# Four sums of operands per pair of row tiles, on GpSimd instead of VectorE

## The chip, the cores and the metric

The kernel runs on one NeuronCore of a Trainium2 chip. The metric is the device time of one execution in microseconds (us). A core has five engines that run their own instruction queues in order and wait for each other by semaphores: TensorE (PE; its weight loads are shown as PEld), VectorE (DVE), ScalarE (ACT), GpSimd (POOL) and SyncE (SP). TensorE writes its results to the banks of PSUM; the other data lies in SBUF.

## The reference, cut to what matters

One decoder layer in float32 over 512 tokens with 1024 channels: a convolution branch and a gated linear attention branch, merged and projected, and then the channel mixer, in which the change lies. There, 1024 channels are projected to 2 x 2816, each of these columns is convolved over time with three taps, the first half goes through silu and is multiplied by the second, and the product is projected back to 1024.

```python
u2 = _rmsnorm(h, norm2_g[l])
z = _causal_dwconv(u2 @ w_ffn_up[l], ffn_dw_w[l], ffn_dw_b[l])
h = h + (jax.nn.silu(z[..., :FFN_DIM]) * z[..., FFN_DIM:]) @ w_ffn_down[l]
return _rmsnorm(h, final_g)
```

## The kernel before

**Precision.** TensorE multiplies in a format with fewer bits than float32, so each operand is split in two: ScalarE copies it to a high part, and VectorE subtracts that from the operand to give the low part. Three matmuls (`mm3`, L309 to L311) then make one product. Weights are split in `split_weight` (copy at L239 or L266, subtraction at L240 or L267; tiles raw, whi, wlo), and the products of the channel mixer in `fsplit` (L1096, L1097; tiles yh and yl, ah and al, sh and sl).

**The channel mixer** goes through 22 row tiles of 128 hidden channels, two by two: 11 pairs in three groups of 4, 3 and 4 pairs (`GROUPS`, L34). For each row tile two up-projections of 24 matmuls fill one PSUM bank each (`col_tile`). `ffn_conv` takes a bank: a bias pass on ScalarE (L1081), and two taps on VectorE (L1083). `glu` multiplies the two halves on VectorE (L1091), to the tile w for the first of a pair and to f for the second.

**Seven products.** The down-projection of a group is not done as eight products of half blocks but as seven, in the manner of Strassen and Winograd, from sums of operands. With w = (w1, w2) and f = (f1, f2), halves of 256 tokens, the sums on the side of the activations are w1 - w2 (L1104), s1 = w2 - f2 (L1114), n2 = s1 - w1 (L1115) and s4 = f1 + n2 (L1116). The first lies in the last third of the tile w, the other three in the tile v. `first_of_pair` splits w1 and w1 - w2 in one copy and one subtraction (yh, yl), and `second_of_pair` splits f (ah, al) and then all of v (sh, sl).

**The products of a group** are made by `seven`, in the order of `STEPS` (L46): a11, a11, a12, s1, a12, s1, then n2, s4, n3 and a22 with two blocks each. The number behind a step picks the first two pairs or the rest of the group. Steps a11 and n3 read y, a12 and a22 read a, and s1, n2 and s4 read s. So the s of a group's last pair is first read in the second block of s1, and its y in the second block of a11. After a step's last block VectorE adds the PSUM bank to the residual (hres, L1019).

**The weights of the seven products** are sums too: `operand` adds one block to another on VectorE (L218), and on GpSimd's queue transfers are issued that accumulate a block from HBM onto a tile (L225 once the tile's split is done, L208 once the tile's first load has landed). SyncE issues the plain loads. Weights are split up to two steps ahead (`LOOK`), in four buffers each for raw, whi and wlo.

**Order.** Outside the start, a scheduler orders each engine's queue when the program is built, by the order in which instructions were written and by when it takes them to be ready. So a line of later code can stand ahead of an earlier one on the same engine. At run time each queue is strictly in order.

GpSimd does few other things: memsets at the start, the roots of the norms (L357, L460, L1152, L1153) and the accumulating transfers.

Of the kernel before, what the change touches and what calls it, by code (L numbers as in the profile page):

```python
# [15 lines left out]
ALU = mybir.AluOpType  # L16
# [3 lines left out]
T = 512  # L20
# [46 lines left out]
def trunk_layer(ctx: ExitStack, tc: tile.TileContext, a: dict, out: bass.AP):  # L67
    nc = tc.nc
# [23 lines left out]
    def nm(s):  # L92
        return f"{s}_{next(names)}"
# [836 lines left out]
    H = T // 2  # L930
# [18 lines left out]
    for p, q in O_PAIRS:  # L949
# [6 lines left out]
        s1, n2, n3, s4 = e1[:, :H], e1[:, H:], e2[:, :H], e2[:, H:]  # L956
# [129 lines left out]
    def glu(i, accs, out):  # L1086

        za = ffn_conv(accs[0], i)
        nc.scalar.activation(za, za, AF.Silu)
        zb = ffn_conv(accs[1], FT + i)  # L1090
        nc.vector.tensor_tensor(out, za, zb, ALU.mult)  # L1091

    def fsplit(src, n, tag):
        hi, lo = (fp.tile([P, n], F32R, tag=tag + p, name=nm(tag + p), bufs=4) for p in "hl")
        shaped = (lambda x: x.rearrange("p (c t) -> p c t", t=H)) if len(src.shape) == 3 else (lambda x: x)
        nc.scalar.copy(shaped(hi), src)  # L1096
        nc.vector.tensor_tensor(shaped(lo), src, shaped(hi).bitcast(F32), ALU.subtract)  # L1097
        return lambda c, n=1: tuple(x[:, c * H : (c + n) * H] for x in (hi, lo))

    def first_of_pair(i, accs):  # L1100

        w = fp.tile([P, 3 * H], F32, tag="w", name=nm("w"), bufs=2)
        glu(i, accs, w[:, :T])
        nc.vector.tensor_tensor(w[:, T:], w[:, :H], w[:, H:T], ALU.subtract)  # L1104
        y = fsplit(w.rearrange("p (c t) -> p c t", t=H)[:, 0:3:2, :], T, "y")
        return w, {"a11": y(0), "n3": y(1)}

    def second_of_pair(i, accs, w, acts):

        f = fp.tile([P, T], F32, tag="f", name=nm("f"), bufs=2)  # L1110
        glu(i, accs, f)
        v = fp.tile([P, 3 * H], F32, tag="v", name=nm("v"), bufs=2)
        s1, n2, s4 = (v[:, c * H : (c + 1) * H] for c in range(3))
        nc.vector.tensor_tensor(s1, w[:, H:T], f[:, H:], ALU.subtract)  # L1114
        nc.vector.tensor_tensor(n2, s1, w[:, :H], ALU.subtract)  # L1115
        nc.vector.tensor_tensor(s4, f[:, :H], n2, ALU.add)  # L1116
        y = fsplit(f, T, "a")
        acts["a12"], acts["a22"] = y(0), y(1)
        y = fsplit(v, 3 * H, "s")
        acts["s1"], acts["n2"], acts["s4"] = y(0), y(1), y(2)  # L1120
        return acts
# [64 lines left out]
    for gi, pairs in enumerate(GROUPS):  # L1186
        acts = []
        early = {}
        if gi == 0:

            ws = [weight("w_up", j, 0) for i in pairs[0] for j in (i, FT + i)]
            accs = [mm_bank() for _ in ws]
            for lo in (0, T // 2):
                for j, (w, acc) in enumerate(zip(ws, accs)):
                    col_tile(w, acts2, acc, lo, lo + T // 2)
                    if lo == 0 and j in (1, 2):
                        to_channels(normed[j + 1], u2, j + 1)
            early = {pairs[0][0]: accs[:2], pairs[0][1]: accs[2:]}

        def both(i):  # L1200
            return early.get(i) or [col_tile(weight("w_up", i), acts2), col_tile(weight("w_up", FT + i), acts2)]

        for p, q in pairs:
            w, found = first_of_pair(p, both(p))
            acts.append(second_of_pair(q, both(q), w, found))
        if gi < len(GROUPS) - 1:
            seven("w_down", pairs, acts, lambda t, n, c: None)
        else:
            seven("w_down", pairs, acts, last_complete, last_at, True)
# [90 lines left out]
```

## Time and profile before

| what | us |
|---|---|
| median of 3 runs | 837.96 |
| lowest and highest of them | 837.56, 837.98 |
| the profiled execution | 837.74 |
| its span, first to last instruction | 836.0 |
| the channel mixer's up-projections and seven products | about 494 to 826 of the span |
| busy in that stretch: TensorE, VectorE, ScalarE, GpSimd | 332.0, 244.5, 154.1, 17.4 |
| the four sums, 44 instructions on VectorE | 18.7 busy (4.7, 4.7, 4.7, 4.6) |

The granted TensorE clock was 0.999 of full speed over the span. A line of the profile's timeline gives the start, the duration, the engine, the line of the kernel, the operation and the tiles (output, arrow, inputs) with their shapes; the time that an engine stood idle before an instruction stands in brackets, with what it waited for. VectorE and TensorE overlap the end of an instruction with the next one's beginning, so what an instruction takes of its queue is the distance of two starts, which is a little less than its duration.

### The profile page before, as it was taken

What the parts mean: (1) busy time and instruction counts of PE and PEld (TensorE: products, weight loads), DVE (VectorE), ACT (ScalarE), POOL (GpSimd) and SP (SyncE); (2) the same over time, 40 slices, a digit from 0 to 9 for tenths busy, and PEclk for the clock granted to TensorE, in tenths of its full rate; (3) what the DMA queues carried; (4) which work ended last, traced back from release to release, by engine and by line L of the source; (5) the groups of instructions that cost most, each with busy time, mean ns of one, the idle gap of its engine ahead of it and who ended that gap; (6) DMA issues with size and microseconds to landing.
All of it is one profiled execution on the core that took longest, in us unless ns stands there. A gap on an engine that the chain in (4) does not pass through costs nothing.

```text
span 836.0 us, 10033 instructions
## 1 busy us (share of the span) xinstructions
PE 826.9 (99%) x3845; PEld 691.3 (83%) x3845; DVE 650.3 (78%) x927; ACT 388.0 (46%) x541; POOL 42.8 (5%) x64
## 2 busy tenths in 40 slices
PE   9999999999999999999999999999999999999996
PEld 7888888888888888888888898888888888888885
DVE  6689979999998798744689858778757787676795
ACT  6633247445543422449444635444434444444454
POOL 2000000000100100000001100001000010000111
PEclk9999999999999999999999999999999999999999
DMA  8232232222222322232348634234842238222462
GB/s 312 102 102 101 101 104 80 101 76 96 82 76 76 127 100 101 76 102 75 114 89 237 190 128 142 88 98 102 217 148 89 69 86 286 102 91 87 101 125 102
DMA packets 28593, 97.79 MB, mean 117 GB/s; under 512 B 3240, under 2 KB 3632, under 8 KB 28544
## 3 DMA queue, kind: packets, MB, share of 16 engines
q1 hardware_dynamic: 25088, 85.35, 29.2%
q0 software_dynamic: 3456, 11.80, 8.1%
q8 instruction: 30, 0.49, 0.2%
q14 instruction: 19, 0.16, 0.1%
HBM read 95.03 MB, written 2.10 MB: 116 GB/s over the span
## 4 chain that ended last, share of the span: by engine, by line
PE 96%; DVE 1%; DMA 1%; issue 0%; ACT 0%; POOL 0%; SPq 0%; POOLq 0%; ACTq 0%
PE mm L309 29%; PE mm L310 29%; PE mm L311 29%; PE mm L519 3%; PE ax L854 1%; PE ax L310 1%; PE ax L309 1%; PE ax L311 1%; DMA x<-in_x_dram 1%; PE ax L856 1%; PE ax L836 1%; PE ax L823 0%; PE ax L871 0%; DVE hres L1019 0%; PE ax L822 0%; PE ax L433 0%
## 5 line engine op out<-in xcount | busy, mean ns | idle before, releaser
L309 PE MATMUL mm<-uh,wlo 128*128 128x512 f32 (+1 forms) x768 | 294.8, 384 | 0.0
L311 PE MATMUL mm<-uh,whi 128*128 128x512 f32 (+1 forms) x768 | 292.4, 381 | 0.0
L310 PE MATMUL mm<-ul,whi 128*128 128x512 f32 (+1 forms) x768 | 292.2, 380 | 0.0
L266 ACT CAST whi<-raw 128x1024 fp32r<-128x1024 f32 x114 | 118.7, 1046 | 129.0 <-PE mm L311 97.2
L311 PEld LDWEIGHTS mm<-uh,whi 128*128 128x128 f32 x768 | 144.4, 188 | 27.8
L309 PEld LDWEIGHTS mm<-uh,wlo 128*128 128x128 f32 x768 | 144.5, 188 | 27.0
L310 PEld LDWEIGHTS mm<-ul,whi 128*128 128x128 f32 x768 | 144.5, 188 | 26.9
L267 DVE TENSOR_TENSOR wlo<-raw,whi 128x1024 fp32r<-128x1024 f32 x114 | 138.3, 1217 | 34.9 <-ACT whi L266 34.8
L613 DVE SCALAR_TENSOR_TENSOR c<-h,pp,c 128x511 f32<-128x511 f32 (+14 forms) x240 | 162.3, 727 | 0.7
L1083 DVE SCALAR_TENSOR_TENSOR tmp<-mm,pp,tmp 128x511 f32<-128x511 f32 x88 | 65.8, 748 | 68.1 <-ACT tmp L1081 67.0
L1081 ACT ACTIVATE tmp<-mm,pp 128x512 f32<-128x512 f32 x44 | 34.3, 780 | 62.6 <-PE mm L311 62.6
L239 ACT CAST whi<-kept 128x1024 fp32r<-128x1024 f32 (+1 forms) x32 | 31.7, 994 | 21.7 <-PE mm L311 9.7
L240 DVE TENSOR_TENSOR wlo<-kept,whi 128x1024 fp32r<-128x1024 f32 (+1 forms) x32 | 36.6, 1152 | 2.5 <-ACT whi L239 2.3
L1019 DVE TENSOR_TENSOR hres<-hres,mm 128x512 f32<-128x512 f32 (+1 forms) x49 | 32.7, 671 | 3.3 <-PE mm L311 2.7
L239 ACT CAST whi<-raw 128x1024 fp32r<-128x1024 f32 (+1 forms) x24 | 23.7, 995 | 20.2 <-PE mm L311 18.7
L240 DVE TENSOR_TENSOR wlo<-raw,whi 128x1024 fp32r<-128x1024 f32 (+1 forms) x24 | 27.3, 1152 | 3.9 <-ACT whi L239 3.8
L310 PE MATMUL mm<-wlo,sh 128*128 128x512 f32 x66 | 25.8, 391 | 0.0
L311 PE MATMUL mm<-whi,sh 128*128 128x512 f32 x66 | 25.7, 389 | 0.0
L309 PE MATMUL mm<-whi,sl 128*128 128x512 f32 x66 | 25.5, 389 | 0.0
L309 PE MATMUL mm<-h,wlo 128*128 128x512 f32 x64 | 25.4, 397 | 0.0
L310 PE MATMUL mm<-h,whi 128*128 128x512 f32 x64 | 24.9, 389 | 0.0
L311 PE MATMUL mm<-h,whi 128*128 128x512 f32 x64 | 24.9, 389 | 0.0
(251 smaller groups left out, 1122.3 us busy)
## 6 DMA issues: line engine op xcount, KB each, us to landing
raw<-in_w_up_dram SPq DMA_DIRECT2D x44, 512.0 KB, 3.5
raw<-in_w_glu_dram SPq DMA_DIRECT2D x16, 512.0 KB, 3.9
raw<-in_w_down_dram SPq DMA_DIRECT2D x15, 512.0 KB, 3.2
kept<-in_w_down_dram POOLq DMA_DIRECT2D x10, 512.0 KB, 5.2
raw<-in_w_v_dram SPq DMA_DIRECT2D x8, 512.0 KB, 3.7
raw<-in_w_qk_dram SPq DMA_DIRECT2D x8, 512.0 KB, 3.2
raw<-in_w_r_dram SPq DMA_DIRECT2D x8, 512.0 KB, 3.3
raw<-in_w_gb_dram SPq DMA_DIRECT2D x8, 512.0 KB, 3.2
```

What stands on the lines that cost most here:

```text
L239: nc.scalar.copy(hi, raw)
L240: nc.vector.tensor_tensor(lo, raw, hi.bitcast(F32), ALU.subtract)
L266: nc.scalar.copy(hi, raw)
L267: pace[0] = nc.vector.tensor_tensor(lo, raw, hi.bitcast(F32), ALU.subtract)
L309: nc.tensor.matmul(acc, ll, rh, start=first, stop=False, **kw)
L310: nc.tensor.matmul(acc, lh, rl, start=False, stop=False, **kw)
L311: nc.tensor.matmul(acc, lh, rh, start=False, stop=last, **kw)
L519: nc.tensor.matmul(acc, act, ready[k // 2][wi][:, j], start=first, stop=last)
L613: nc.vector.scalar_tensor_tensor(y[:, s:], c[:, : T - s], w, y[:, s:], ALU.mult, ALU.add)
L1019: nc.vector.tensor_tensor(hres[t, n][:, c], hres[t, n][:, c], bank[of[step]][i][:, c], op)
L1081: nc.scalar.activation(z, acc, AF.Identity, bias=pp[:, PP_FB + m : PP_FB + m + 1], scale=w[2])
L1083: nc.vector.scalar_tensor_tensor(z[:, s:], acc[:, : T - s], w[j], z[:, s:], ALU.mult, ALU.add)
```

## The change

The four sums of operands in `first_of_pair` and `second_of_pair` are issued on GpSimd, with the same operands, outputs and operations. Nothing else is changed; the order of the queues is made anew by the scheduler.

```diff
         w = fp.tile([P, 3 * H], F32, tag="w", name=nm("w"), bufs=2)
         glu(i, accs, w[:, :T])
-        nc.vector.tensor_tensor(w[:, T:], w[:, :H], w[:, H:T], ALU.subtract)
+        nc.gpsimd.tensor_tensor(w[:, T:], w[:, :H], w[:, H:T], ALU.subtract)
         y = fsplit(w.rearrange("p (c t) -> p c t", t=H)[:, 0:3:2, :], T, "y")
         return w, {"a11": y(0), "n3": y(1)}
...
         s1, n2, s4 = (v[:, c * H : (c + 1) * H] for c in range(3))
-        nc.vector.tensor_tensor(s1, w[:, H:T], f[:, H:], ALU.subtract)
-        nc.vector.tensor_tensor(n2, s1, w[:, :H], ALU.subtract)
-        nc.vector.tensor_tensor(s4, f[:, :H], n2, ALU.add)
+        nc.gpsimd.tensor_tensor(s1, w[:, H:T], f[:, H:], ALU.subtract)
+        nc.gpsimd.tensor_tensor(n2, s1, w[:, :H], ALU.subtract)
+        nc.gpsimd.tensor_tensor(s4, f[:, :H], n2, ALU.add)
         y = fsplit(f, T, "a")
```

## The prediction

> **What bounds the kernel now.** I read the page's busy times first, then the waits of TensorE, then the timeline around the changed instructions, and last what GpSimd's rows cost.
>
> ```profile
> PE 826.9 (99%) x3845; PEld 691.3 (83%) x3845; DVE 650.3 (78%) x927; ACT 388.0 (46%) x541; POOL 42.8 (5%) x64
> PE 96%; DVE 1%; DMA 1%; issue 0%; ACT 0%; POOL 0%; SPq 0%; POOLq 0%; ACTq 0%
> ```
>
> TensorE is busy for 826.9 of 836.0 us and is 96% of the chain that ended last. In the list of who waited for whom TensorE has four lines, 2.3 us together, and none lies in the channel mixer between 494 and 826 us. The columns of the next view are the stretch, its length, and busy time with number of instructions by engine; I chose the ends of the first two groups, where the seven products run.
>
> ```profile
> 571.00:609.00 38.00, 38.00 (x169) 31.46 (x169) 30.04 (x36) 16.45 (x17) 3.46 (x4) 1.00 0.67 177
> 674.00:703.00 29.00, 29.00 (x129) 23.77 (x128) 25.90 (x36) 12.91 (x17) 3.42 (x4) 1.00 0.69 199
> ```
>
> TensorE has no gap there, but VectorE is at 79% and 89%. So VectorE's work is hidden, with little left over just where the last pair of a group is made ready. VectorE's timeline at the end of the first group (start, duration, line, operation, tiles):
>
> ```profile
> 574.66 0.68 DVE L1091 TENSOR_TENSOR f<-tmp,tmp 128x512 f32<-128x512 f32 x1
> ...
> 575.86 0.42 DVE L1114 TENSOR_TENSOR v<-w,f 128x256 f32<-128x256 f32 x1
> 576.19 1.22 DVE L218 TENSOR_TENSOR kept<-kept,raw 128x1024 f32<-128x1024 f32 x1
> 577.33 0.42 DVE L1115 TENSOR_TENSOR v<-v,w 128x256 f32<-128x256 f32 x1
> ...
> 578.26 0.42 DVE L1116 TENSOR_TENSOR v<-f,v 128x256 f32<-128x256 f32 x1
> ...
> 580.33 0.95 DVE L1097 TENSOR_TENSOR sl<-v,sh 128x768 fp32r<-128x768 f32 x1
> ...
> 586.82 1.22 DVE L240 TENSOR_TENSOR wlo<-kept,whi 128x1024 fp32r<-128x1024 f32 x1
> ```
>
> The reader is to see that VectorE runs without a break from the last product f to the weight split at 586.82 (one gap of 0.30 us at 585.92). That split, the second block of step n2, ends at 588.04; TensorE first reads it here:
>
> ```profile
> 588.96 0.39 PE L310 MATMUL mm<-wlo,sh 128*128 128x512 f32 x1
> ```
>
> The cover is 588.96 - 588.04 = 0.9 us. In the last group the same split ends at 806.92 and is read at about 808.1 (n2 starts 12 matmuls of 0.227 us after 803.83, and the read comes 7 matmuls later): 1.2 us. In the second group n2's first split (685.91 to 687.14) is read by the second matmul after 686.66, and TensorE's starts there run 0.53 and 0.33 us where 0.45 and 0.227 are usual: the cover is zero and some 0.2 us is lost already. Everything else has more: sl (ends 581.3) is read at 585.34 by the matmuls of the last pair.
>
> **What the change removes.** 44 VectorE instructions of 0.42 us (11 each at L1104, L1114, L1115, L1116). Back to back each takes 0.34 us of the queue (575.86 to 576.19, 577.33 to 577.66, 578.26 to 578.60), so 44 x 0.34 = 15 us of the 244.5 us that VectorE is busy from 494 to 826. Off the path this is worth nothing; per group end it frees 3 x 0.34 = 1.0 us of VectorE's unbroken stretch.
>
> **What it adds.** 44 GpSimd subtractions and additions of 128x256, which the trace doesn't show. These rows stand nearest:
>
> ```profile
> L712 POOL MEMSET tmp<- 128x512 f32 x1 | 0.5, 528 | 56.4 <-DVE h L621 56.4
> masks.py:197 POOL MEMSET ident<- 128x128 f32 x1 | 0.2, 204 | 0.3 <-POOLq L1287 0.3
> 467.34 0.57 POOL L357 TENSOR_TENSOR rstd<-var,mhalf 128x1 f32<-128x1 f32 x1 [10.26 <-DVE var L1040]
> 471.30 1.41 POOL L357 TENSOR_TENSOR rstd<-var,mhalf 128x1 f32<-128x1 f32 x1 [3.40 <-DVE var L1040]
> 816.57 0.18 POOL L1152 TENSOR_TENSOR var<-ss,var 128x1 f32<-128x1 f32 x1 [8.37 <-ACT junk L1137]
> ```
>
> An addition of one column takes 0.18 us, and a column costs (528 - 204)/384 = 0.84 ns in a memset. If each of two operands costs as much, 256 columns take 0.18 + 2 x 256 x 0.84 ns = 0.61 us. The low bound is one pass, 0.40 us. For the high bound, compare the two rows of L357: the same operation takes 0.57 us alone and 1.41 us when VectorE runs a 1.22 us subtraction of two SBUF tiles at 471.07; it ends 0.42 us after that one. So GpSimd can be held up for a VectorE instruction: at most 1.22 us more, 1.83 us. The Trainium skill, page "SBUF — State Buffer", section "Who interferes with whom", says that a VectorE instruction with two SBUF inputs and a GpSimd instruction that reads SBUF exclude each other for the whole instruction, whichever came first; the row agrees for GpSimd as the loser, and no row here shows VectorE as the loser. I take 0.61 us with waiting in both directions.
>
> By the Trainium skill, page "GPSIMD Engine Reference", section "Elementwise — side-by-side cycle accounting", an addition of 2048 float32 columns takes 4497 ns on GpSimd, about 0.56 us for 256, an estimate to which the 0.18 us above would be added: 0.74 us. By that price the sum below would be some 0.4 us higher.
>
> **Inside the groups** the sum of L1104 stands before ScalarE's copy yh, which waits for it and has the bias pass L1081 of the next tile queued behind it. At 521 us yh ends about 0.2 us later (0.61 for 0.42), and L1081 already waits 0.24 us for TensorE. Cost zero; what hides it is that weights are split two tiles (2 x 5.45 us) ahead. Without that cover it would be 11 x 0.2 = 2 us.
>
> **At a group end**, first group: L1114 at 575.4 to 576.0 under the residual sum hres, which reads PSUM; L218 held 0.15 us, to 577.2; L1115 to 577.8 after it; al, held for it, to 578.5; L1116 to 579.1; ScalarE's copy sh from 579.15 instead of 578.72. VectorE meanwhile does hres and the split at 579.20, so sl starts at 580.33 as before. VectorE's stretch: -1.0 + 0.15 + 0.6 = about -0.25 us. Cost zero, under 0.9 us of cover; the last group alike, under 1.2 us. In the second group f ends at 678.69, and the same steps give L1116 to 681.3, sh to 682.2, sl at 682.5 instead of 682.62: zero if VectorE's order stays as it is. If the instruction order puts sl ahead of the two splits at 681.42 and 682.02, VectorE stands idle for up to 1.0 us, and there this goes to TensorE one for one. I take 0.3 us, a third of it.
>
> **GpSimd's queue** also issues the accumulating transfers (L208, L225; 0.86 us each). The one at 564.28 meets the last pair's L1104 (w is ready at 564.5): whichever is second is up to 0.9 us late. yl is then ready by 567.2 and read at 574.5; the transfer's target is split at 579.5. The other issues, at 573.32 and 583.97, lie before f and after the last sum. Zero.
>
> **Sum.** 836.0 + 0 + 0.3 + 0 = 836.3 us of span; the profiled run took 837.74, 1.74 more than its span, and the median of the runs shown, 837.96, is 0.22 above it. 838.3 us.
>
> **Rivals.** (1) *The relief is a gain:* VectorE's freed 1.0 us closes the second group's lost 0.2 us. More cannot come, since TensorE waits for nothing else there: 837.96 - 0.2 = 837.8 us. For it speaks the 89%; against it, that the sums come later than before. (2) *The chain of three sums becomes the bound,* slower: f, three sums in a row, sh, sl, and behind sh and sl the weight splits of s1 and n2 on both queues. If each sum takes 1.5 us with its waits (between 0.61 and 1.83), the last ends at 581.65 instead of 578.68, sl at 583.7, and the split at 586.82 ends 2.1 us late, at 590.2: 1.2 us beyond its cover, as much less 0.3 in the last group and 2.1 in the second, 4.2 us together, 837.96 + 4.2 = 842.2 us. It decides from about 0.9 us a sum (VectorE's stretch then grows past 0.9 us), and costs more than 1.7 us in all from about 1.2 us a sum. For it speaks the 1.41 us row; against it, that a back-to-back run of 0.66 us VectorE instructions at 279.5 let GpSimd in at its first boundary. (3) *The order on GpSimd's queue:* a transfer that waits for landed data (L208 at 584.68) is put ahead of a sum. L1116 then ends at 586.3, sl at 588.2, 2.8 us after its first use at 585.34; with 2.8 and about 3.3 in the other groups 8.9 us, 846.9 us. Against it: the sums are ready 5 us earlier. That the change does not do what it says is no rival: the engine is written out in each of the four lines.
>
> **How the numbers follow.** Forecast 0.52; (1) 0.07; (2) 0.34; (3) 0.05; 0.02 for a gain that no row prices. The bound of 0.2%, about what a measurement of this kernel can tell from no change, is 1.7 us. Forecast and (1) lie within it: 0.59. Slower are (2) and (3): 0.39. Faster is the unpriced gain: 0.02. The range goes from 837.4 (rival 1 less the runs' spread of 0.4) to 843.2 (rival 2 at 1.6 us a sum, some 0.3 us more in each of three groups); what is left out is rival 3, the top of rival 2 (1.6 to 1.83 us a sum) and the unpriced gain. The forecast's own range is 837.6 to 839.6.
>
> **What would show it.** TensorE without new gaps near 588.96, 686.7 and 808; GpSimd's rows of 128x256 near 0.6 us alone and below 1.9 us held; VectorE some 15 us less busy; sh within 0.5 us of its old place. I am wrong if TensorE waits for sl, or for a split behind it, at the group ends, if the order of VectorE's or GpSimd's queue puts such work late, or if the sums cost over 1 us.

## The result and the profile after

The changed kernel takes 840.66 us (median of 8 runs, 839.85 to 841.75) against 837.97 us (8 runs, 837.56 to 839.07) of the kernel before. The ratio is 1.0031 with a 95% interval of 1.0023 to 1.0040: slower by 2.7 us, which is over the bound of 0.2% (1.7 us). The profiled execution took 840.52 us with a span of 838.8 us, 2.8 us more than before. The page of the changed kernel, busy time by engine and the chain that ended last:

```profile
PE 828.1 (99%) x3845; PEld 691.0 (82%) x3845; DVE 636.8 (76%) x883; ACT 386.5 (46%) x541; POOL 80.9 (10%) x108
PE 88%; DVE 5%; issue 2%; DMA 2%; ACT 2%; POOL 2%; POOLq 0%; SPq 0%; ACTq 0%
```

VectorE is 13.5 us less busy and GpSimd 38 us more. TensorE's share of the chain falls from 96% to 88%: work of VectorE, ScalarE and GpSimd now stands in it. The two group ends that were shown before, by stretch (length, then busy time of TensorE, weight loads, VectorE, ScalarE, GpSimd):

```profile
571.00:609.00 38.00, 37.69 (x167) 30.86 (x166) 29.80 (x33) 16.01 (x17) 6.87 (x7) 1.00 0.65 175
674.00:703.00 29.00, 27.95 (x121) 22.24 (x120) 24.03 (x32) 12.60 (x16) 6.00 (x7) 1.00 0.64 176
```

TensorE was busy without a gap in both; now 0.3 and 1.05 us are missing, and VectorE has become less busy in the second, 24.0 for 25.9 us. So VectorE is idle where TensorE waits. Its timeline at the end of the first group, with GpSimd's and the copy on ScalarE:

```profile
574.46 0.68 DVE L1091 TENSOR_TENSOR f<-tmp,tmp 128x512 f32<-128x512 f32 x1
575.06 0.68 DVE L1019 TENSOR_TENSOR hres<-hres,mm 128x512 f32<-128x512 f32 x1
575.66 1.39 DVE L218 TENSOR_TENSOR kept<-kept,raw 128x1024 f32<-128x1024 f32 x1
576.98 1.22 DVE L1097 TENSOR_TENSOR al<-f,ah 128x512 fp32r<-128x512 f32 x1
579.70 0.96 DVE L1097 TENSOR_TENSOR sl<-v,sh 128x768 fp32r<-128x768 f32 x1 [1.49 <-ACT sh L1096]
580.57 0.68 DVE L1019 TENSOR_TENSOR hres<-hres,mm 128x512 f32<-128x512 f32 x1
581.17 1.22 DVE L240 TENSOR_TENSOR wlo<-raw,whi 128x1024 fp32r<-128x1024 f32 x1
```

```profile
575.24 0.73 POOL L1114 TENSOR_TENSOR v<-w,f 128x256 f32<-128x256 f32 x1 [0.37 <-DVE f L1091]
576.05 1.60 POOL L1115 TENSOR_TENSOR v<-v,w 128x256 f32<-128x256 f32 x1
577.73 1.06 POOL L1116 TENSOR_TENSOR v<-f,v 128x256 f32<-128x256 f32 x1
```

```profile
578.83 0.83 ACT L1096 CAST sh<-v 128x768 fp32r<-128x768 f32 x1 [2.11 <-POOL v L1116]
```

The reader is to compare the order with that of before, where these rows stood ahead of sl (580.33), and where TensorE first read the split:

```profile
578.60 0.68 DVE L1019 TENSOR_TENSOR hres<-hres,mm 128x512 f32<-128x512 f32 x1
579.20 1.22 DVE L240 TENSOR_TENSOR wlo<-raw,whi 128x1024 fp32r<-128x1024 f32 x1
...
582.16 0.39 PE L310 MATMUL ax<-wlo,ah 128*128 128x512 f32 x1
```

sl even starts 0.6 us earlier than then (579.70 for 580.33), but these two instructions, hres and the weight split of the second a12 block, now stand behind it. VectorE is idle for 1.49 us at the head of its queue, waiting for sh, while that split could have run: its copy whi was done at 576.2. The split ends at 582.39, for 580.42 before, which was 1.74 us ahead of its read. At the other two ends sl waits as long; in the second group it is the first split of n2 that comes late (687.30 for 685.91), in the last again that of a12:

```profile
682.81 0.96 DVE L1097 TENSOR_TENSOR sl<-v,sh 128x768 fp32r<-128x768 f32 x1 [1.50 <-ACT sh L1096]
...
687.30 1.23 DVE L240 TENSOR_TENSOR wlo<-kept,whi 128x1024 fp32r<-128x1024 f32 x1
...
801.16 0.96 DVE L1097 TENSOR_TENSOR sl<-v,sh 128x768 fp32r<-128x768 f32 x1 [1.49 <-ACT sh L1096]
...
802.63 1.22 DVE L240 TENSOR_TENSOR wlo<-raw,whi 128x1024 fp32r<-128x1024 f32 x1
```

TensorE waits for the late splits (the first and the second end are shown; the last is like the first), and in the second group's a22 for a residual sum:

```profile
582.44 0.50 PE L310 MATMUL ax<-wlo,ah 128*128 128x512 f32 x1 [0.31 <-DVE wlo L240]
...
688.58 0.50 PE L310 MATMUL mm<-wlo,sh 128*128 128x512 f32 x1 [0.76 <-DVE wlo L240]
...
701.12 0.47 PE L309 MATMUL mm<-whi,al 128*128 128x512 f32 x1 [0.22 <-DVE hres L1019]
```

The waits in brackets are shorter than what is lost, since a matmul's end is drawn late: those that start 0.227 us apart are drawn 0.39 us long. The loss is read better by laying the starts of the same 3845 matmuls of the two profiles beside each other. The changed kernel is 0.19 us ahead when the first group ends, and then behind: 0.43 us after the first group's end, 1.62 us after n2 of the second group, 2.09 us after its a22, 2.74 us after the last group's end, and 2.75 us when TensorE ends. So the losses are 0.62, 1.18, 0.47 and 0.65 us: 2.9 us at the three group ends, and nothing in between. The 0.47 us at a22 has another path than the rest: the chain that ended last goes there through a transfer onto a weight tile, issued at 690.13, that took 8.8 us to land.

The chain of waits of the changed kernel in order of time (start, duration; pieces under 0.1 us left out) names the steps of the first loss:

```profile
574.46 0.69 DVE f L1091
575.24 0.74 POOL v L1114
576.05 1.60 POOL v L1115
577.73 1.07 POOL v L1116
578.83 0.84 ACT sh L1096
579.73 0.84 issue
580.57 0.68 DVE hres L1019
581.25 1.15 DVE wlo L240
582.44 0.50 PE ax L310
```

It is rival 2's chain, from f to a weight split, but it reaches TensorE through the split that stands behind sl. The 0.84 us of "issue" are the time that sl took of the queue, with hres behind it.

### The profile page after: what moved, and what is told of

Its sections match the earlier page's. It is cut to its first block, busy times and chain, and to the rows that moved or that the text cites. A ratio compares the mean times of both kernels' runs of the same rounds, so it can differ in the third digit from the quotient of the medians.

```text
span 838.8 us, 10045 instructions
## 1 busy us (share of the span) xinstructions
PE 828.1 (99%) x3845; PEld 691.0 (82%) x3845; DVE 636.8 (76%) x883; ACT 386.5 (46%) x541; POOL 80.9 (10%) x108
## 4 chain that ended last, share of the span: by engine, by line
PE 88%; DVE 5%; issue 2%; DMA 2%; ACT 2%; POOL 2%; POOLq 0%; SPq 0%; ACTq 0%
PE mm L309 26%; PE mm L311 26%; PE mm L310 26%; PE mm L519 3%; DVE wlo L240 2%; DVE hres L1019 1%; DMA kept<-in_w_down_dram 1%; PE ax L854 1%; PE ax L856 1%; PE ax L836 1%; ACT junk L1137 1%; POOL v L1115 0%; PE ax L823 0%; PE ax L871 0%; PE ax L433 0%
## 5 line engine op out<-in xcount | busy, mean ns | idle before, releaser
L357 POOL TENSOR_TENSOR rstd<-var,mhalf 128x2 f32<-128x2 f32 (+1 forms) x12 | 12.2, 1024 | 219.7 <-DVE var L861 196.3
L1097 DVE TENSOR_TENSOR sl<-v,sh 128x768 fp32r<-128x768 f32 x11 | 10.5, 957 | 20.6 <-ACT sh L1096 20.6
```

## The experiments

Three theories were held against each other. A: the loss lies at the three group ends, where sl stands at the head of VectorE's queue, its input late, with weight splits behind it. B: GpSimd's reads and VectorE's hold each other up, and the loss is spread over all pairs, or, in a second form, this holding is what matters at the group ends. C, formed later: what A's repair leaves is the holding. Each time is set against 26 to 35 runs of the kernel before, with a median of 837.85 to 837.88 us.

**Where: the last pairs alone, and all but these.** One line chooses the engine of a pair's four sums; the other run has the two engines the other way round.

```diff
         for p, q in pairs:
-            w, found = first_of_pair(p, both(p))
-            acts.append(second_of_pair(q, both(q), w, found))
+            eng = nc.gpsimd if (p, q) == pairs[-1] else nc.vector
+            w, found = first_of_pair(p, both(p), eng)
+            acts.append(second_of_pair(q, both(q), w, found, eng))
```

> Only the last pair of each of the three groups has its four sums on GpSimd (12 of 44 instructions). Theory A (at the three group ends sl stands at the head of VectorE's queue and the weight splits wait behind it): nearly the whole loss stays, 840.4 to 840.9 us, VectorE idle some 1.5 us ahead of sl three times, TensorE late by 0.6, 1.6 and 0.7 us. Theory B (each GpSimd sum holds VectorE up by the shared reads, and the loss is spread over all 11 pairs): 3/11 of 2.7 us, 838.7 us.

> The other eight pairs have their four sums on GpSimd (32 of 44 instructions), the last pair of each group on VectorE. Theory A: no loss, 837.8 to 838.2 us, although VectorE still idles ahead of yl and sl in those pairs. Theory B: 8/11 of 2.7 us, 839.9 us.

The last pairs alone: 840.5 us, ratio 1.0031 (1.0019 to 1.0043). All but these: 838.32 us, 0.1 us over A's range, ratio 1.0006 (0.9998 to 1.0015, so at most 1.3 us). The loss goes with 12 of the 44 instructions, and the other 32 cost nothing that the measurement can tell. In the first profile TensorE's starts fall back by 0.65, 1.17 and 0.67 us at the three ends, the second less than the 1.6 us expected, since nothing is lost at a22. In that second profile VectorE still idles ahead of its splits (last two numbers: idle time before the group, and what ended it):

```profile
L1097 DVE TENSOR_TENSOR sl<-v,sh 128x768 fp32r<-128x768 f32 x11 | 10.5, 954 | 16.1 <-ACT sh L1096 16.1
```

16 us of idle VectorE cost nothing here: TensorE's starts stay within 0.1 us of those of before from one end of the channel mixer to the other. This fits weights that are split two tiles ahead. At the group ends of the changed kernel 1.5 us, three times, go with 2.5 of the 2.9 us. B in its first form falls.

**The holding by itself: GpSimd makes every sum a second time.** The sums on VectorE stay; GpSimd's go into a tile that nobody reads.

```diff
         nc.vector.tensor_tensor(s4, f[:, :H], n2, ALU.add)
+        nc.gpsimd.tensor_tensor(dup(), w[:, H:T], f[:, H:], ALU.subtract)
+        nc.gpsimd.tensor_tensor(dup(), s1, w[:, :H], ALU.subtract)
+        nc.gpsimd.tensor_tensor(dup(), f[:, :H], n2, ALU.add)
```

(and the same behind L1104, where dup() stands for a new tile of 128x256)

> The sums that count stay on VectorE; GpSimd makes all 44 a second time, into a tile that nobody reads. So GpSimd's reads meet VectorE's as in the changed kernel, but nothing waits for them and VectorE's order is that of before. Theory A: VectorE is held up to 0.5 us per instruction, about 1 us per group end, which the first and last group cover (0.9 and 1.2 us) and the second does not: 838.0 to 839.0 us. Theory B, and its form in which the holding matters at the group ends alone: 840 us or more.

839.97 us, ratio 1.0025 (1.0016 to 1.0035): 1 us over A's range, and 0.03 us below what B expected. VectorE's rows at the first group's end (the sums' lines are moved down by the edit, L1115 to L1117):

```profile
575.89 0.66 DVE L1115 TENSOR_TENSOR v<-w,f 128x256 f32<-128x256 f32 x1
...
577.60 0.96 DVE L1116 TENSOR_TENSOR v<-v,w 128x256 f32<-128x256 f32 x1
...
579.09 0.96 DVE L1117 TENSOR_TENSOR v<-f,v 128x256 f32<-128x256 f32 x1
```

The three sums take 0.66, 0.96 and 0.96 us for 0.42 each, and of the queue, from start to start, 0.58, 0.88 and 0.88 us for 0.33 or 0.34: VectorE loses 1.3 us at the first and the last end, not the 1 us of the expectation, and 1.0 us at the second. TensorE's starts fall back by 0.3, 1.0 and 0.3 us at the three ends, close to what the cover of 0.9, 0 and 1.2 us leaves of it, and by 0.4 us in the tail, where TensorE waits for a residual sum; the cause of the last was not followed up. So VectorE does lose when GpSimd came first, and this costs time where nothing is taken off VectorE in return. In the changed kernel 1.0 us is taken off per group end. The run leaves B's second form standing for part of the loss, and the next ones decide on that.

**The order repaired: all sums on GpSimd, sl behind the weight split.** The split of v of a group's last pair is put off (L1119) and written inside `seven`, after the weight split that stood ahead of it before.

```diff
                 parts.append((1, weight(name, (pairs, step, 1))))
+            if late_split and (step, d) == ("a12", 0):
+                late_split.pop()()
             half, n, op, whole = into[step]
...
+        if late:
+            late_split.append(split_sums)
```

> The changed kernel, with one thing moved: the split of v (sh, sl) of a group's last pair is written after the weight split of the second a12 block, so that sl stands behind that split on VectorE, as it did before. All 44 sums stay on GpSimd. Theory A: the idle time ahead of sl shrinks from 1.5 us to below 0.3 us in the first and last group, and the time falls to 837.9 to 838.9 us. Theory B and its group-end form: the holding is the same, 840 us or more.

838.43 us, ratio 1.0005 (0.9996 to 1.0013). With every GpSimd sum in place and as long as in the changed kernel (0.73, 1.60 and 1.07 us at the first end), the loss is gone at the first and the last end. VectorE at the first end:

```profile
577.03 1.22 DVE L1101 TENSOR_TENSOR al<-f,ah 128x512 fp32r<-128x512 f32 x1
578.18 0.68 DVE L1023 TENSOR_TENSOR hres<-hres,mm 128x512 f32<-128x512 f32 x1
578.78 1.21 DVE L240 TENSOR_TENSOR wlo<-raw,whi 128x1024 fp32r<-128x1024 f32 x1
579.91 0.94 DVE L1101 TENSOR_TENSOR sl<-v,sh 128x768 fp32r<-128x768 f32 x1
```

al is still held up, 1.22 us for 0.69, yet no idle time stands ahead of sl, and TensorE has no gap at 582. So with the price of the sums and the holding unchanged, moving sl behind the split takes the loss away there. In the second group TensorE still loses 0.6 us more than before; two further edits put the line one and two steps later, at ("s1", 0) and ("a12", 1). The code reads the second a12 block after the first s1 block, so the last of the two is the latest.

> As the run with the split of v behind the second a12 weight split, but written behind the split of the second s1 block as well. All 44 sums on GpSimd. Theory A: the idle time of 0.35 us that was left ahead of sl in the second group goes, and of the 0.5 us left of TensorE's loss there some 0.1 to 0.3 us remain: 837.9 to 838.4 us. Theory C (what was left is the holding of VectorE by GpSimd's sums): it stays at 838.4 us or more.

> The split of v of a group's last pair is written behind the first n2 weight split, so that in the second group sl also stands behind the sum L218 on which that split waits. All 44 sums on GpSimd. Theory A: in the second group n2's split ends ahead of its read at 686.9, and the 0.2 us go that the kernel before lost there: 837.5 to 838.0 us, no slower than before. Theory C: 838.4 us or more. If sl becomes too late for the second s1 block instead, TensorE waits for sl, and the time is over 839 us.

One step later: 838.52 us, 1.0003 (0.9995 to 1.0012), not to be told from the run ahead of it by its time, 0.1 us over A's range and so within C's. In the profile TensorE's loss in the second group falls from 0.7 and 0.1 us at two matmuls to 0.2 and 0.1 us. Two steps later: 837.80 us, 0.9997 (0.9989 to 1.0006), the same as before, with 44 sums on GpSimd. VectorE at the second group's end of this run:

```profile
680.70 1.22 DVE L240 TENSOR_TENSOR wlo<-raw,whi 128x512 fp32r<-128x512 f32 x1
681.85 0.68 DVE L240 TENSOR_TENSOR wlo<-kept,whi 128x512 fp32r<-128x512 f32 x1
682.45 1.21 DVE L218 TENSOR_TENSOR kept<-kept,raw 128x1024 f32<-128x1024 f32 x1
683.59 0.94 DVE L1101 TENSOR_TENSOR sl<-v,sh 128x768 fp32r<-128x768 f32 x1
...
685.05 1.21 DVE L240 TENSOR_TENSOR wlo<-kept,whi 128x1024 fp32r<-128x1024 f32 x1
```

The split that TensorE waited for starts at 685.05, for 687.30 in the changed kernel and 685.91 before, although the first split is held to 1.22 us for 0.68. C falls. The later split was not run with the sums on VectorE, so it isn't measured whether it would gain there too; in this profile TensorE gains 0.2 us at most on the kernel before at the three group ends. No version came out faster than the kernel before by more than the interval.

**The order alone: all sums on VectorE, the split held behind sl.**

```diff
                 nc.scalar.copy(hi, raw)
-                nc.vector.tensor_tensor(lo, raw, hi.bitcast(F32), ALU.subtract)
+                with ExitStack() as held:
+                    if name == "w_down" and spec[1:] == ("a12", 1):
+                        held.enter_context(tc.issue_after(last_sl[0].ins))
+                    nc.vector.tensor_tensor(lo, raw, hi.bitcast(F32), ALU.subtract)
```

(`last_sl[0]` is the latest subtraction of `fsplit`, here the sl of the group's last pair.)

> The kernel before, all sums on VectorE, with one ordering edge: the weight split of the second a12 block stands behind the sl of the group's last pair, as in the changed kernel. Theory A: VectorE's sums are ready earlier than GpSimd's, so the idle time ahead of sl is about 0.4 us in the first and last group (covered) and 0.4 to 1.0 us in the second (not covered): 838.3 to 839.0 us. If the order alone cost what the change cost, whatever makes the sums: 840 us or more.

838.20 us, 0.1 us below A's range, ratio 1.0003 (0.9995 to 1.0011): the interval holds no loss and one of 0.9 us. VectorE idles 0.31 us ahead of sl at the first end, for 1.49 in the changed kernel (the edit moves the lines down by 4):

```profile
580.44 0.96 DVE L1101 TENSOR_TENSOR sl<-v,sh 128x768 fp32r<-128x768 f32 x1 [0.31 <-ACT sh L1100]
581.31 1.22 DVE L244 TENSOR_TENSOR wlo<-raw,whi 128x1024 fp32r<-128x1024 f32 x1
```

The split starts 5.81 us after f (575.50) here, 4.54 us after it in the kernel before and 6.71 us in the changed kernel. So the order alone makes it 1.3 us late, within its cover of 1.74 us, and the order with late sums 2.2 us, beyond it; TensorE loses nothing at the first and the last end of this run. This profile ends 0.9 us behind that of before, but 1.0 us arises at 478 us, ahead of the channel mixer and of the weights that the edit touches. Both are needed then at these two ends: sums that come late, and weight splits queued behind what waits for them. For the second group, where most is lost, the run can't say it: there the edge also moved L218 ahead of sl, so it is not the changed kernel's order in full, and n2's split came earlier than before.

**The first sum alone on GpSimd.** L1104 as in the change, the rest as before.

> Only the sum in first_of_pair is made by GpSimd (11 of 44 instructions); the three sums of v stay on VectorE. Theory A (the loss is the place of sl in VectorE's queue at the group ends, ahead of weight splits while its input is late): sl's chain is untouched, no loss, 837.7 to 838.2 us. Theory B (GpSimd's reads hold VectorE up, spread over the instructions): 11/44 of 2.7 us, 838.6 us.

838.82 us, ratio 1.0006 (0.9998 to 1.0015): 0.6 us over A's range by the median and near B's 838.6 us, and the interval does not separate the two. The group ends are as before but for one place: the second group's a22 is 0.5 us late at 699.65, where a transfer of 256 KB issued at 688.82 (before: 688.73) landed after 8.6 us (before: 7.0). The changed kernel has 8.8 us there, and 0.47 us of its loss. Whether the sums have a part in this landing stays open; the run with the order repaired had 6.9 us with all sums on GpSimd.

## Why the prediction was right or wrong

The measured time lies inside the range, and on the other side of the 0.2% bound from the likeliest case: 2.7 us where 0.3 us was forecast. The range reaches so far only for rival 2, which had the sign but not the way in which the time was lost, so that it holds the time is in part luck. The prediction's own sign of being wrong came: TensorE waits at the group ends for a split behind sl. Step by step:

- **What bounds the kernel** was right: cover of about 1 us at the first and the last group end, none at the second. All of the loss stands at these three places, largest at the second. At the first and the last the late split was not that of n2, whose cover was worked out, but that of a12, which had 1.74 us.
- **What is removed** was right: VectorE's stretch loses its three sums, and this is worth nothing off the path.
- **The price of a sum** was too low: 0.61 us was taken; the group of L1114, which nothing holds up, has 0.73 us. The estimate of 0.74 us from the Trainium skill's "GPSIMD Engine Reference", section "Elementwise — side-by-side cycle accounting" (4497 ns for 2048 columns, with 0.18 us of a row here added), agrees with the trace.
- **The holding** works in both directions, as was assumed. L1115 takes 1.60 us where L218 came first, and al 1.22 us for 0.68 where L1115 came first. This is what the Trainium skill's "SBUF — State Buffer", section "Who interferes with whom", states, and the trace agrees with VectorE as the loser as well. It rests within the bounds given, 0.40 to 1.83 us: the three sums had 0.73, 1.60 and 1.06 us at the first end, on average 1.13 us, and 0.73, 0.74 and 1.06 us at the second, on average 0.84 us. Price and holding together came out as reckoned: from the end of f to that of the last sum 3.65 us at the first end (575.14 to 578.79), for 3.76 us in the prediction, and sh started at 578.83, for 579.15.
- **The step that failed:** "VectorE meanwhile does hres and the split at 579.20, so sl starts at 580.33 as before", and "zero if VectorE's order stays as it is". The order did not stay. The case that sl moves ahead of the splits was seen, but for the second group alone, and priced there at a third of 1.0 us. It came at all three ends, with 1.5 us of idle time each: 0.6 + 1.2 + 0.7 us for 0 + 0.3 + 0. The other 0.5 us, at the second group's a22, followed a late landing that has no term in the sum. The runs with the order repaired keep the price and the holding, and the loss goes; these two still have a part in it, since they make sl's input late.
- **Rival 2** had the chain and the sign, 4.2 us at 1.5 us a sum. By its own decision point, more than 1.7 us lost from about 1.2 us a sum, the loss came too soon: 2.7 us at 1.13 us a sum on average, and the most in the second group, at 0.84 us. Its way to TensorE was another: it took the loss to come from a chain that is too long, through n2's second split, where at the first end sl came 0.6 us earlier than before and the a12 split behind it was late. Its 581.65 can't be redone either: three sums of 1.5 us from the end of f at 575.34 end at 579.84.
- **Rival 1** could not show: n2's lost 0.2 us in the second group went in the profiles of the latest split and of the order alone, and lies within their intervals. **Rival 3** did not come: the transfers on GpSimd's queue came ahead of the sums or well after them.
- **Inside the groups** zero was right: 32 sums and 16 us of idle VectorE time there cost nothing that can be told.

## What to carry to other kernels

When an operation moves to another engine, its consumer keeps its place in a queue that is strictly in order, or gets a new one: ask what the order will be when the input comes later, and what then stands behind the waiting consumer. Work taken off a busy engine is worth nothing if that engine then waits at the head of its queue for the same result; here 1.0 us of work went and 1.5 us of idle time came. Where a scheduler sets the order at build time, the remedy can be to write the consumer later, behind the work that has a nearer due time; here this cost nothing that the measurement can tell.

## What the runs showed of the hardware

GpSimd's subtraction of two float32 tiles of 128x256 takes 0.73 us alone, for 0.42 us on VectorE. When VectorE runs an instruction on two SBUF tiles, whichever comes second waits for the whole of the first: GpSimd's sum went to 1.60 us behind a 1.2 us sum, and VectorE's 0.42 us sum to 0.96 us behind GpSimd's. A VectorE sum with one operand in PSUM was not held: hres kept its 0.68 us beside L1114, which kept its 0.73 us. Sums that nobody reads, run only beside the others, cost 2.1 us of the kernel, 1.6 us of it at the group ends.
